# The gate stage of a product-key expert layer: one of its two one-hot products made by ScalarE instead of VectorE

## The chip, the cores and the metric

The kernel runs on one core of a Trainium2 chip. The metric is the device time of one execution in microseconds. Three runs of the kernel before took 2521.78, 2525.56 and 2527.47 us; their median is 2525.56 us.

## The reference

The program runs two blocks of two layers each on 256 tokens of width 1024. The first block (gated delta rule, retention, SwiGLU) is not touched. Each layer of the second block mixes the tokens (a linear recurrence beside sparse attention) and then applies a layer of experts. Only the experts matter here:

```python
q = (xf @ wq).reshape(T, 8, 2, 128)
s = jnp.einsum('thcd,ckd->thck', q, subkeys)
sv, si = lax.top_k(s, 16)                      # 16 best of 128 keys, twice
cand = (sv[:, :, 0, :, None] + sv[:, :, 1, None, :]).reshape(T, 8, 256)
cv, ci = lax.top_k(cand, 16)
experts = ea * 128 + eb                        # 8 heads x 16 experts a token, of 16384
gate = softmax(cv)
act = gelu(einsum('cd,ced->ce', xc, u_tab[experts]))
y = einsum('ce,ced->cd', act * gate, v_tab[experts])
```

Every token picks 128 of 16384 experts. Its output is the sum over these experts of gelu(x . u) times the gate times v.

## The kernel before

160 of the 256 tokens (`DENSE`) are computed densely. All 16384 products x . u are made in 128 units of 128 experts each (`u_unit`), multiplied by a gate table that is zero where an expert was not picked, and multiplied by v in 128 further steps (`v_part`). One unit and one `v_part` step are eight fp32 products of 128x128 by 128x160 each (16 matmul records in the profile). Each reads 128x1024 fp32 weights, half of a 1 MB load by the SP queue into the tiles `raw` (3 buffers) or `ru` (2).

The other 96 tokens (`FEW`) are computed by gathering the rows of u and v that they picked: `few_tokens` issues indirect DMAs from GpSimd, 128 rows of 1024 fp32 at a time (called a row batch below), into a ring of five tiles `frow`. VectorE reduces each u batch against x (line 1589) and adds each v batch to a sum (line 1595), and the tile is then free for the next gather. A layer has 192 such batches: 96 of u, then 96 of v.

The layer goes through these stages:

- Scores and first units: ten units are made ahead (`FIRST`).
- Ranks and top k: VectorE finds the experts; `pace` weaves units between.
- Gate stage (`gbuild`, line 1830): 40 steps of four tokens ("quads"). In a step VectorE writes two one-hot tables (`gAB`, line 1838: 128 picks in partitions, 128 first keys and 128 second keys in columns, four tokens innermost), and then the second one-hot times the gate (`gB2`, line 1840). The gate is held as two fp16 numbers, a high half and the remainder, so `gB2` has two halves. TensorE multiplies the first one-hot by both halves (line 1850: eight matmuls a quad), which sums the gates into a 128x128 table a token in PSUM. This is done one step late (`late`). VectorE (line 1857) multiplies the units that are already made by that table, and ScalarE (line 1859) copies the rest of the table out, to be multiplied when the unit comes.
- In each step `pace(self.QUAD)` runs `both`: one row batch, and then as many units as fit. A counter `spare` grows by `QUAD` and falls by `UNIT` = 2.2 with each unit; units are made while it is above zero. A unit in this stage is finished by a gelu on ScalarE (lines 1564 and 1567, split where the table already stands) and a product on VectorE (line 1565).
- V stage (in `peer_units`): 128 `v_part` steps (line 1666). The units that are still missing are spread over the first 96 steps, and the row batches over all steps, except the last eight (`HELD`). Then `peer_end` transposes the dense result, adds the sums of the gathered tokens (line 1712) and normalizes.

The order of instructions on each engine is fixed when the program is built. It follows the program's order, but a planner with its own costs lets an instruction go ahead where an earlier one is not ready by its reckoning. `tc.issue_after(self.mark)` keeps a row batch's VectorE instruction behind the quad's `gB2`.

Of the kernel before, what the change touches and what calls it, by code (L numbers as in the profile page):

```python
# [221 lines left out]
F32 = mybir.dt.float32  # L222
# [4 lines left out]
AF = mybir.ActivationFunctionType  # L227
ALU = mybir.AluOpType
# [25 lines left out]
class Body:  # L254
# [1220 lines left out]
    RANK = 1.0  # L1475
    TOP = 1.3
    DEC = 5.0
    QUAD = 2.2

    def peer(self, l):  # L1480

        nc, tc, I = self.nc, self.tc, self.I
        N, FEW = self.DENSE, self.FEW
        with tc.tile_pool(name="pz", bufs=1) as Z:
            self.few_pool = Z
            hk = Z.tile([128, 4, N], F16, name="hk")
            hf = Z.tile([128, 8, 256], F32, name="hf")
            groups = []  # L1490
            for g, (n, first) in enumerate(FEW):
                few = Z.tile([128, n], U32, name=f"fidx{g}")
                fg = Z.tile([128, n], F32, name=f"fgate{g}")
                fs = Z.tile([128, n], F32, name=f"fs{g}")
                fx = Z.tile([128, 1024], F32, name=f"fx{g}", tag=f"fx{g}")
                pair = Z.tile([128, n], F32, name=f"fpair{g}")
                if n == 64:
                    nc.vector.tensor_add(pair, self.ident[:, 0:64], self.ident[:, 64:128])
                else:
                    nc.vector.tensor_reduce(pair, self.ident.rearrange("p (r n) -> p n r", n=n), axis=mybir.AxisListType.X,  # L1500
                                            op=ALU.add)
                groups.append((n, first, few, fg, fs, fx, pair))
            sums = {}
            self.x_to_h(hf)
            with tc.tile_pool(name="pt", bufs=1) as P, tc.tile_pool(name="pm0", bufs=1) as M:
                prod = [M.tile([128, self.SPLIT, N], F32, name="prod0")]

                def u_products(w):
                    p = self.ps([128, N])
                    for k in range(8):  # L1510
                        nc.tensor.matmul(p, w[:, k * 128:(k + 1) * 128], hf[:, k, 0:N], start=(k == 0), stop=(k == 7))  # L1511
                    return p

                with tc.tile_pool(name="uf", bufs=self.FIRST // 2) as UF:
                    early = []

                    def ahead(i):
                        if i % 2 == 0 and 4 <= i < 4 + self.FIRST:
                            early.append(self.load_pair(I["pu"][l, (i - 4) // 2], UF))

                    with tc.tile_pool(name="hlw", bufs=2) as self.HL, tc.tile_pool(name="psw", bufs=2) as W:
                        best, rest = self.scores(l, P, W, ahead, prod[0].rearrange("p b t -> p (b t)")[:, -2048:])
                        self.settle()
                        for n, first, few, fg, fs, fx, pair in groups:
                            for s in range(0, 128, n):
                                nc.scalar.activation(fx[s:s + n, :], self.X[first:first + n, 1, :], AF.Copy)
                        for b in range(self.FIRST):
                            nc.scalar.activation(prod[0][:, b, :], u_products(early[b // 2][:, b % 2, :]), AF.Gelu_apprx_tanh)
                with tc.tile_pool(name="pm", bufs=1) as M:
                    prod.append(M.tile([128, 128 - self.SPLIT, N], F32, name="prod1"))  # L1530
                    self.peer_units(l, P, M, groups, sums, hk, u_products, best, rest, prod)
            with tc.tile_pool(name="pe", bufs=1) as W:
                self.peer_end(l, W, groups, sums)
# [284 lines left out]
    def turn(self, W, out, hk, ti, n):  # L1818


        nc = self.nc
        p = self.ps([128, 3, 128], "a")
        for z in range(3):
            nc.tensor.transpose(p[:, z, :], out[:, z, :], self.ident)
        t = slice(ti * 128, ti * 128 + n)
        nc.scalar.activation(hk[:, 0:2, t], p[:, 0:2, 0:n], AF.Copy)
        nc.scalar.activation(hk[:, 2, t], p[:, 2, 0:n], AF.Copy, scale=GATE_UNIT)
        nc.vector.scalar_tensor_tensor(hk[:, 3, t], p[:, 2, 0:n], GATE_UNIT, hk[:, 2, t], op0=ALU.mult, op1=ALU.subtract)

    def gbuild(self, W, iota4, hk, prod, state, pace):  # L1830

        nc, SPLIT = self.nc, self.SPLIT
        late = None
        for quad in range(self.DENSE // 4):
            t = slice(quad * 4, quad * 4 + 4)
            AB = W.tile([128, 2, 128, 4], F16, name="gAB")
            B2 = W.tile([128, 2, 128, 4], F16, name="gB2")
            nc.vector.tensor_tensor(AB, iota4[:, None].to_broadcast([128, 2, 128, 4]),
                                    hk[:, 0:2, None, t].to_broadcast([128, 2, 128, 4]), op=ALU.is_equal)
            self.mark = nc.vector.tensor_tensor(B2, AB[:, 1, None].to_broadcast([128, 2, 128, 4]),  # L1840
                                                hk[:, 2:4, None, t].to_broadcast([128, 2, 128, 4]), op=ALU.mult).ins
            if late is not None:
                late()
            pace(self.QUAD)

            def late(AB=AB, B2=B2, t=t):
                p = self.ps([128, 4, 128], "a")
                for j in range(4):
                    for i in range(2):
                        nc.tensor.matmul(p[:, j, :], AB[:, 0, :, j], B2[:, i, :, j], start=(i == 0), stop=(i == 1))  # L1850
                pv = p.rearrange("p t b -> p b t")
                made = state["made"]
                for i, (lo, hi) in enumerate(((0, SPLIT), (SPLIT, 128))):
                    m = min(max(made, lo), hi)
                    if m > lo:
                        d = prod[i][:, 0:m - lo, t]
                        nc.vector.scalar_tensor_tensor(d, pv[:, lo:m, :], 1.0 / GATE_UNIT, d, op0=ALU.mult, op1=ALU.mult)
                    if m < hi:
                        nc.scalar.activation(prod[i][:, m - lo:hi - lo, t], pv[:, m:hi, :], AF.Copy, scale=1.0 / GATE_UNIT)
                state["built"] = t.stop  # L1860
        late()
# [99 lines left out]
```

## Time and profile before

| | us |
|---|---|
| median of three runs | 2525.56 |
| profiled execution | 2522.34 |
| its span, first to last instruction | 2520.5 |
| TensorE busy | 2395.2 |
| VectorE busy | 1634.2 |
| ScalarE busy | 794.1 |
| GpSimd busy | 443.6 |

The span leaves out 1.84 us of the execution's own time. Matmuls are pipelined and their ends are modelled, so that the starts of TensorE's instructions tell its pace better than their lengths do. The two expert layers' gate stages lie at about 1129 to 1257 us and 1967 to 2090 us of the span, their V stages at 1257 to 1658 us and 2090 to 2497 us.

### The profile page before, as it was taken

The page shows a single profiled execution, that of the slowest core. Times are in us where ns is not written, and L with a number is a line of the kernel's source. Part 1 is how long each engine was busy: PE and PEld are TensorE (multiplying, and loading weights), DVE is VectorE, ACT ScalarE, POOL GpSimd, SP SyncE. Part 2 cuts the span into 40 slices and gives each one's busy share as a digit, 9 for nine tenths or more (in the row PEclk, how much of TensorE's full clock was granted, in tenths as well). Part 3 has the DMA queues.
Part 4 walks back from the last instruction along what each step waited for, and adds up shares of the span by engine and source line. Part 5 has one row for each costly group of instructions (what it writes and reads, how often), then busy time and mean ns, then how long its engine had stood idle before and what let it go on. Part 6 is the DMA issues. An engine that isn't in the chain of part 4 may idle for free. (4 is left out here: it accounts for less than half of the span.)

```text
span 2520.5 us, 42374 instructions
## 1 busy us (share of the span) xinstructions
PE 2395.2 (95%) x16994; PEld 2254.1 (89%) x16994; DVE 1634.2 (65%) x3427; ACT 794.1 (32%) x1653; POOL 443.6 (18%) x425
## 2 busy tenths in 40 slices
PE   5998999999999999999999999979999999999996
PEld 4887998977899887999999999958799999999995
DVE  6877886745555566989944444466589795444445
ACT  5464444344444456522200000034753220000000
POOL 0000000000000000033333233420002333333343
PEclk8999999999999999999999999989999999999998
DMA  7735996444455623579999999983265999999997
GB/s 289 254 132 198 328 333 240 152 163 163 144 198 184 198 89 132 200 298 333 330 397 415 412 415 406 407 294 114 86 236 216 349 336 375 415 415 416 413 406 296
DMA packets 153781, 704.38 MB, mean 279 GB/s; under 512 B 14704, under 2 KB 15600, under 8 KB 120176
## 3 DMA queue, kind: packets, MB, share of 16 engines
q1 hardware_dynamic: 97712, 498.43, 52.8%
q0 software_dynamic: 55296, 201.35, 20.7%
q8 instruction: 134, 2.20, 0.3%
q10 hardware_dynamic: 576, 1.89, 0.2%
q14 instruction: 63, 0.52, 0.1%
HBM read 700.57 MB, written 1.05 MB: 278 GB/s over the span
## 5 line engine op out<-in xcount | busy, mean ns | idle before, releaser
L1666 PE MATMUL ps_a<-prod,raw 128*128 128x160 f32 x4096 | 576.8, 299 | 7.4 <-DMA raw<-in_pv_dram 6.1
L1666 PEld LDWEIGHTS ps_a<-prod,raw 128*128 128x128 f32 x4096 | 562.7, 190 | 9.3 <-issue 6.8
L308 DVE TENSOR_TENSOR wlo<-raw,whi 128x1024 fp32r<-128x1024 f32 x316 | 385.5, 1223 | 249.2 <-ACT whi L306 245.1
L306 ACT ACTIVATE whi<-raw 128x1024 fp32r<-128x1024 f32 x316 | 333.2, 1058 | 389.1 <-PE ps_r L331 162.8
L1595 DVE SCALAR_TENSOR_TENSOR fa<-frow,fs,fa 128x1024 f32<-128x1024 f32 x188 | 241.5, 1284 | 277.9 <-DMA frow<-in_pv_dram,fidx 269.2
L330 PE MATMUL ps_r<-hh,whi 128*128 128x256 f32 x1376 | 393.6, 287 | 6.2 <-ACT whi L306 2.4
L331 PE MATMUL ps_r<-hh,whi 128*128 128x256 f32 x1376 | 390.8, 284 | 3.1 <-DVE hh L437 2.5
L332 PE MATMUL ps_r<-hh,wlo 128*128 128x256 f32 x1376 | 390.0, 284 | 2.6 <-DVE wlo L308 2.6
L1511 PE MATMUL ps_r<-hf,ru 128*128 128x160 f32 x2560 | 373.2, 299 | 0.0
L1511 PEld LDWEIGHTS ps_r<-hf,ru 128*128 128x128 f32 x2560 | 356.0, 190 | 0.1
L1589 DVE SCALAR_TENSOR_TENSOR frow<-frow,fx 128x1024 f32<-128x1024 f32 x192 | 233.7, 1220 | 126.4 <-DMA frow<-in_pur_dram,fidx 126.1
L1577 POOL DMA_INDIRECT frow<-in_pur_dram,fidx x192 | 208.2, 1084 | 571.0 <-DVE frow L1589 268.3
L1564 ACT ACTIVATE gelu<-ps_r 128x160 f32<-128x160 f32 (+10 forms) x192 | 53.0, 277 | 700.8 <-PE ps_r L1511 661.3
L330 PEld LDWEIGHTS ps_r<-hh,whi 128*128 128x128 f32 x1376 | 263.3, 192 | 10.2 <-ACT whi L306 2.9
L331 PEld LDWEIGHTS ps_r<-hh,whi 128*128 128x128 f32 x1376 | 263.5, 191 | 8.1 <-DVE hh L437 6.0
L332 PEld LDWEIGHTS ps_r<-hh,wlo 128*128 128x128 f32 x1376 | 263.1, 191 | 3.9 <-DVE wlo L308 3.8
L1577 POOL DMA_INDIRECT frow<-in_pv_dram,fidx x192 | 195.0, 1016 | 360.8 <-DVE fa L1595 186.0
L1511 PE MATMUL ps_r<-hf,raw 128*128 128x160 f32 x1536 | 225.2, 304 | 7.8 <-ACT prod L1567 6.1
L1511 PEld LDWEIGHTS ps_r<-hf,raw 128*128 128x128 f32 x1536 | 216.4, 194 | 8.9 <-ACT prod L1567 6.6
L1850 PE MATMUL ps_a<-gB,gAB 128*128 128x128 f16 x640 | 88.3, 295 | 0.0
L1565 DVE TENSOR_TENSOR prod<-prod,gelu 128x160 f32<-128x160 f32 (+10 forms) x192 | 55.4, 288 | 40.7 <-ACT gelu L1564 37.3
L1850 PEld LDWEIGHTS <-gAB 128*128 128x128 f16 x640 | 72.9, 116 | 2.6
(490 smaller groups left out, 3080.5 us busy)
## 6 DMA issues: line engine op xcount, KB each, us to landing
raw<-in_pv_dram SPq DMA_DIRECT2D x128, 1024.0 KB
ru<-in_pu_dram SPq DMA_DIRECT2D x80, 1024.0 KB
raw<-in_pu_dram SPq DMA_DIRECT2D x48, 1024.0 KB
raw<-in_ffn_in_dram SPq DMA_DIRECT2D x44, 1024.0 KB
adr<-in_ada_dram SPq DMA_DIRECT2D x56, 512.0 KB
raw<-in_ffn_out_dram SPq DMA_DIRECT2D x22, 1024.0 KB
raw<-in_ada_dram SPq DMA_DIRECT2D x20, 1024.0 KB
raw<-in_ret_tm_dram SPq DMA_DIRECT2D x16, 1024.0 KB
```

The costliest lines, as they stand in the source:

```text
L306: self.last_hi = self.nc.scalar.activation(hi[:, :n], src, AF.Copy)
L308: self.last_split = self.nc.vector.tensor_sub(lo[:, :n], src, hi[:, :n].bitcast(F32))
L330: nc.tensor.matmul(out, a, self.hhi[:, k, :], start=(k == 0), stop=False)
L331: nc.tensor.matmul(out, a, self.hlo[:, k, :], start=False, stop=False)
L332: nc.tensor.matmul(out, b, self.hhi[:, k, :], start=False, stop=(k == 7))
L1511: nc.tensor.matmul(p, w[:, k * 128:(k + 1) * 128], hf[:, k, 0:N], start=(k == 0), stop=(k == 7))
L1565: self.gated = nc.vector.tensor_mul(at(b)[:, 0:t], at(b)[:, 0:t], g[:, 0:t])
L1577: nc.gpsimd.indirect_dma_start(out=r, out_offset=None, in_=I["pv" if z else "pur"], in_offset=bass.IndirectOffsetOnAxis(groups[g][2][:, j: ...
L1589: nc.vector.scalar_tensor_tensor(r, r, 1.0, fx, op0=ALU.mult, op1=ALU.mult, accum_out=fs[:, j:j + 1])
L1595: nc.vector.scalar_tensor_tensor(fa, r, fs[:, j:j + 1], fa, op0=ALU.mult, op1=ALU.add)
L1666: nc.tensor.matmul(acc[c // 2][:, c % 2, :], v[:, c * 128:(c + 1) * 128], at(b), start=(b == 0 and c % 2 == 0), stop=(b == 127), skip_grou ...
L1850: nc.tensor.matmul(p[:, j, :], AB[:, 0, :, j], B2[:, i, :, j], start=(i == 0), stop=(i == 1))
```

## The change

`turn` also keeps the high half of the gate as fp32 (`hk2`, one more ScalarE copy in each of its two calls a layer). In `gbuild` VectorE makes only the low half of `gB2`. ScalarE makes the high half with four instructions a quad, one for each token: a copy of the second one-hot (128x128, every fourth element) with `hk2`'s column as the scale of each partition. `QUAD`, the pace of units, goes from 2.2 to 1.9.

```diff
-    QUAD = 2.2
+    QUAD = 1.9
...
             hk = Z.tile([128, 4, N], F16, name="hk")
+            self.hk2 = Z.tile([128, N], F32, name="hk2")
...
         nc.scalar.activation(hk[:, 2, t], p[:, 2, 0:n], AF.Copy, scale=GATE_UNIT)
+        nc.scalar.activation(self.hk2[:, t], hk[:, 2, t], AF.Copy)
...
-            self.mark = nc.vector.tensor_tensor(B2, AB[:, 1, None].to_broadcast([128, 2, 128, 4]),
-                                                hk[:, 2:4, None, t].to_broadcast([128, 2, 128, 4]), op=ALU.mult).ins
+            self.mark = nc.vector.tensor_tensor(B2[:, 1], AB[:, 1], hk[:, 3, None, t].to_broadcast([128, 128, 4]),
+                                                op=ALU.mult).ins
+            for j in range(4):
+                nc.scalar.activation(B2[:, 0, :, j], AB[:, 1, :, j], AF.Copy, scale=self.hk2[:, quad * 4 + j:quad * 4 + j + 1])
```

## Rows read from the trace of the kernel before

**Rows 1.** Page: busy time by engine, and what the DMA moved in 40 equal slices.
```profile
PE 2395.2 (95%) x16994; PEld 2254.1 (89%) x16994; DVE 1634.2 (65%) x3427; ACT 794.1 (32%) x1653; POOL 443.6 (18%) x425
...
GB/s 289 254 132 198 328 333 240 152 163 163 144 198 184 198 89 132 200 298 333 330 397 415 412 415 406 407 294 114 86 236 216 349 336 375 415 415 416 413 406 296
```

**Rows 2.** Windows: gate stage, two V stages. Columns: PE, PEld, DVE, ACT, POOL, PEclk, DMA, GB/s.
```profile
1129.30:1256.70 127.40, 127.40 (x982) 126.03 (x981) 115.20 (x263) 32.09 (x140) 44.25 (x40) 1.00 0.92 332
1256.70:1655.00 398.30, 394.67 (x2899) 393.61 (x2898) 182.98 (x243) 17.95 (x61) 133.01 (x134) 1.00 1.01 408
...
2090.00:2488.00 398.00, 394.24 (x2899) 393.36 (x2898) 184.84 (x251) 18.75 (x63) 137.24 (x135) 1.00 1.01 410
```

**Rows 3.** Chain of waits in time order: start, length, what held the chain.
```profile
1995.17 2.18 PE ps_r L1511 x16
1997.35 0.94 PE ps_a L1850 x8
...
2090.52 1.14 DVE frow L1589 x2
...
2252.97 13.09 DMA frow<-in_pv_dram,fidx
2266.16 1.28 DVE fa L1595
...
2503.00 4.93 PE ps_r L1712 x6
```

**Rows 4.** Timeline, first half of a gate stage: start, length, engine, instruction.
```profile
1175.24 0.69 DVE L1838 TENSOR_TENSOR gAB<-iota,hk 128x1024 f16<-128x1024 f16 x1
...
1176.37 0.68 DVE L1840 TENSOR_TENSOR gB<-gAB,hk 128x1024 f16<-128x1024 f16 x1
...
1178.37 0.69 DVE L1838 TENSOR_TENSOR gAB<-iota,hk 128x1024 f16<-128x1024 f16 x1
...
1178.83 1.11 PE L1850 MATMUL ps_a<-gB,gAB 128*128 128x128 f16 x8
```

**Rows 5.** Timeline, last third of the same gate stage, VectorE.
```profile
1241.10 0.30 DVE L1565 TENSOR_TENSOR prod<-prod,gelu 128x140 f32<-128x140 f32 x1
...
1244.21 0.31 DVE L1565 TENSOR_TENSOR prod<-prod,gelu 128x144 f32<-128x144 f32 x1
```

**Rows 6.** Groups by shape, VectorE: changed instruction, and 16-bit ones of other lengths.
```profile
L1840 DVE TENSOR_TENSOR gB<-gAB,hk 128x1024 f16<-128x1024 f16 x80 | 54.6, 682 | 0.0
...
L1807 DVE TENSOR_TENSOR teq<-teq 128x512 bf16<-128x512 bf16 x8 | 3.3, 417 | 0.0
...
L1807 DVE TENSOR_TENSOR teq<-teq 128x256 bf16<-128x256 bf16 x8 | 2.2, 280 | 0.0
```

**Rows 7.** Groups by shape, ScalarE: 128x128 without and with a per-partition operand.
```profile
L434 ACT ACTIVATE fmf<-ps_r,par 128x256 f32<-128x256 f32 x8 | 3.9, 575 | 1.4 <-PE ps_r L424 1.4
L830 ACT ACTIVATE vb<-ps_a,gbv 128x128 f32<-128x128 f32 x8 | 2.3, 367 | 0.0
L799 ACT ACTIVATE ktok<-ps_a,gbg 128x128 f32<-128x128 f32 x4 | 1.2, 408 | 0.0
L1827 ACT ACTIVATE hk<-ps_a 128x128 f16<-128x128 f32 x2 | 0.5, 271 | 0.0
```

**Rows 8.** Timeline: four ScalarE instructions with per-partition operands back to back.
```profile
1685.31 1.93 ACT L434 ACTIVATE fmf<-ps_r,par 128x256 f32<-128x256 f32 x4 [1.36 <-PE ps_r L424]
```

**Rows 9.** TensorE's waits in the two V stages and their ends.
```profile
PE ps_a L1666 <- DMA raw<-in_pv_dram: 3.0, 3, 1.9
...
PE ps_r L1712 <- DVE fa L1595: 4.7, 1, 4.7
PE ps_a L1666 <- DMA raw<-in_pv_dram: 3.1, 3, 2.1
```

**Rows 10.** Timeline, end of layer 0's V stage.
```profile
1650.67 7.84 PE L1666 MATMUL ps_a<-prod,raw 128*128 128x160 f32 x56 [1.91 <-DMA raw<-in_pv_dram]
...
1669.57 3.95 DVE L1595 SCALAR_TENSOR_TENSOR fa<-frow,fs,fa 128x1024 f32<-128x1024 f32 x3 [1.04 <-DMA frow<-in_pv_dram,fidx]
```

## The prediction

> **What bounds the kernel now.** I read the page first. TensorE is busy for 95% of the span, so whatever the change does elsewhere counts only through TensorE or through the ends of the two expert layers. The GB/s row shows the second thing to see: 333, 330 and 336 in the slices of the gate stages (19, 20 and 33), about 415 for the rest of both layers [rows 1]. Then I cut both layers into stages by windows. In layer 0's gate stage TensorE shows no idle time at all in 127.4 us, VectorE is busy for 115.2, ScalarE for 32.1, and DMA moves 332 GB/s. In the V stages TensorE is busy 394.7 of 398.3 and 394.2 of 398.0 us, DMA moves 408 to 410 GB/s, and its busy share is 1.01: both are full at once [rows 2].
>
> The chain of waits says which of the two ends last. Through the gate stage it runs on TensorE alone: 2.18 us for one unit of u, 0.94 us for a quad's eight gate matmuls. From 2090 us on it leaves TensorE for good and runs through the gathers: a gather takes 13.09 us to land, VectorE adds it in 1.28 us, that frees a ring tile, and so on to the last sum, which the pair product at 2503.00 waits for [rows 3]. Five tiles at 13.09 + 1.28 us give 2.87 us a row batch; the 144 batches that are left after the gate stage (192 less 40 in it and 8 before it) would take 414 us at that pace, and 2090 to 2503 is 413. So the end of a layer is the end of the gathers, and these are slow because the weights share a full DMA with them. The waits agree: TensorE waits 4.7 us for the last sum in layer 1, and 3.0 and 3.1 us for v weights [rows 9]. In layer 0 the last v product ends at 1658.5 and the last sum at 1673.5 [rows 10].
>
> **The change, part by part.**
>
> *Units.* From the code: 40 quads by 2.2 / 2.2 give 40 units in the gate stage; 40 by 1.9 / 2.2 = 34.5 give 35. Five units a layer move to the V stage, which then has 62 + 128 products instead of 57 + 128. At 2.18 us [rows 3] that takes 5 x 2.18 = 10.9 us of TensorE out of the gate stage and puts 10.9 us into the V stage: nothing for TensorE as a whole. Each unit brings its 0.524 MB weights along (128 x 1024 x 4 bytes), 2.62 MB a layer.
>
> *VectorE.* A quad's step was 3.13 us in the first half (start to start of line 1838 [rows 4]) and 3.11 us in the last third, where VectorE is packed [rows 5]. The halved product was not seen at its new size: it is 128x512 of fp16 instead of 128x1024 at 0.682 us. Bounds are 0.280 (128x256 bf16) and 0.682; the nearest is the 128x512 bf16 product, 0.417 [rows 6]. It saves 0.265 us a quad: 3.11 becomes 2.85 where VectorE is packed.
>
> *ScalarE.* Four instructions a quad of 128x128 with a scale per partition, SBUF to SBUF in fp16 with a stride, a form that no row shows. Without such an operand 128x128 takes 0.271 us, with one 0.367 to 0.408, so four cost 1.08 to 1.63 us [rows 7]. Back to back they overlap: four of 0.575 took 1.93 rather than 2.30 [rows 7, 8], so I take 4 x 0.367 less 3 x 0.12 = 1.1 us. ScalarE goes from 32.1 / 40 = 0.80 [rows 2] to about 1.9 us a quad, 2.4 at the upper bound, of a step of 2.85. It is not the bound, but 67 to 85% full and in order.
>
> Does the longer way to `gB2` delay the gate matmuls? They run one step late. The product of 1176.37 ends at 1177.05, its one-hot at 1175.93 [rows 4]; the matmuls that use it start at 1178.83 [rows 4]. ScalarE may begin at 1175.93 and needs 1.1 to 1.6 us, so it is done by 1177.6 with over a microsecond in hand. That hides it. Queued behind the four are the copy of the last table (line 1859) and the gelu of the unit, on which line 1565 on VectorE waits in order: where the four get in ahead of a gelu, VectorE stands still for up to 1.1 us. I count that at nothing on the mean, and it is the main risk. The extra copy in `turn`, some 0.3 us, twice a layer, is not in front of the one-hot, and units cover it.
>
> The Trainium skill speaks against the move: "ScalarE: Activation LUTs", section Rules for kernel authors, gives multiplications to VectorE rather than ScalarE. The rows agree as far as work goes (1.1 us added for 0.265 taken off); by that rule the step would lengthen wherever ScalarE is waited for, which is the slower rival below.
>
> *The gate stage.* TensorE needs 0.94 + 35/40 x 2.18 = 2.85 us a quad, VectorE 2.85 at its fullest. 40 quads took 127.4 us [rows 2]; less 10.9 it is 116.5 (2.91 a quad).
>
> *The V stage and the sum.* The gathers start their 144 batches 10.9 us earlier. Against that, DMA has 2.62 MB more to move while it is full: 2.62 MB / 415 GB/s [rows 1] = 6.3 us. Net -4.6 us a layer: the gain is DMA time that the gate stage left unused. If the planner lets units run ahead (of 982 matmuls in the gate stage [rows 2] 320 are the quads', and 662 make 41.4 units, not 40), and twice as many do so after, 3.6 units instead of 5 leave: 7.8 - 4.5 = -3.3 us a layer. Two layers give -9.2 to -6.6; I take the middle, -7.9. The profiled execution (span 2520.5, with 1.84 us around it 2522.34) would go to about 2514.4. It lay 3.2 us under the median, so against the median I say 2525.56 - 7.9 = 2517.7.
>
> **The rivals.**
>
> *Nothing moves (2525.6, 2522 to 2529).* TensorE is 99% busy or more in each window [rows 2], and the change takes no matmul away. The planner places row batches by the count of products made, so gathers may be held to TensorE's pace and start no batch earlier. Against it: VectorE waits for gathers, not the other way, and the chain from 2090 on does not touch TensorE [rows 3].
>
> *The gate stage does not get shorter (slower, 2538).* VectorE waits in order for a gelu behind the four, or the gate matmuls wait for the high half, and the step stays at 127.4 / 40 = 3.19 us with fewer units in it. Then 6.3 us of DMA a layer are added and nothing returned: +12.6, 2538. Were TensorE the bound in the V stage it would be +21.8, 2547. The point where it turns is a gate stage 6.3 us shorter, 121.1 us, 3.03 us a quad: a mean stall of 0.12 us over my 2.91 undoes the gain. For it: both engines are near 2.85 together, and ScalarE over two thirds full. Against it: matmuls of later units can fill TensorE, as they did before.
>
> *The gathers take it all (faster, 2507).* If weights go on at the old share of DMA, gathers end 10.9 us sooner in layer 0, where there is 15 us between last v product and last sum [rows 10], and up to 4.7 + 3.1 us sooner in layer 1 [rows 9]: -18.7, 2507.
>
> **How the numbers follow.** My forecast (-5 to -13) has 0.48, no change 0.22, the stage that does not shorten 0.22, the gathers that take all 0.08. About 0.2%, 5 us, is what a measurement of this kernel tells from no change. Faster is the first but 0.01 at its edge, with the last, 0.55; within 0.2% is the second and that edge, 0.23; slower is the third, 0.22. The likeliest case alone spans 2512 to 2521. The range for 8 in 10 goes from the last rival's 2507 to 2533, which takes in no change and the first part of the slower case and leaves the rest of it out.
>
> **What the profile after would show.** Right: line 1840 near 0.42 us, ScalarE's four near 0.37 each, matmuls of line 1850 about 2.9 us from quad to quad, the gate stages 8 to 11 us shorter with TensorE still without idle time, 62 gelus in each V stage, and v waits on weights no longer than before. Wrong: idle time before line 1850 released by ScalarE, VectorE waiting for gelu by tens of microseconds, quads at 3.03 us or more; or a shorter gate stage with the last sum where it was, which would say that the gathers do not set the end.

## The result and the profile after

The changed kernel takes 2499.29 us (median of five runs, 2494.03 to 2501.72), against 2525.56 us before (2521.78 to 2531.53 over five runs): a ratio of 0.9898, 95% interval 0.9884 to 0.9913. That is 26 us less, where 7.9 were forecast, and below the forecast's range of 2507 to 2533. The profiled execution took 2501.52 us, with a span of 2499.7.

The page of the changed kernel shows the trade that was meant, and one thing more: the chain that ended last has changed hands. The first line is busy time by engine, the second what DMA moved in 40 slices, the third the chain's share of the span by engine, and the last two are groups of instructions (count, busy time in us, mean of one in ns, then the engine's idle time before them).

```profile
PE 2387.4 (96%) x16994; PEld 2247.0 (90%) x16994; DVE 1609.7 (64%) x3421; ACT 897.7 (36%) x1971; POOL 491.9 (20%) x425
...
GB/s 290 253 135 194 328 319 254 154 160 162 161 183 175 216 87 100 254 251 354 342 410 416 414 415 415 390 303 128 89 242 215 371 338 399 415 414 415 414 390 306
...
PE 20%; DVE 3%; DMA 2%; issue 1%; ACT 0%; POOL 0%; POOLq 0%; DVEq 0%
...
L1566 DVE TENSOR_TENSOR prod<-prod,gelu 128x160 f32<-128x160 f32 (+9 forms) x192 | 56.8, 296 | 367.9 <-ACT gelu L1565 357.7
...
L1845 ACT ACTIVATE gB<-gAB,hk 128x128 f16<-128x128 f16 x320 | 121.0, 570 | 19.7 <-DVE gAB L1840 17.2
```

Before, the chain's shares were:

```profile
DMA 12%; PE 8%; DVE 4%; issue 2%; POOL 1%; ACT 0%; POOLq 0%; DVEq 0%; ACTq 0%
```

ScalarE gained 103.6 us of work and VectorE lost 24.5 [rows 1]. TensorE, which computes the same, was busy 7.8 us less: its matmuls themselves ran faster somewhere. DMA moves 354 and 342 GB/s in the slices of layer 0's gate stage (the second reaches 7 us into the V stage), where it moved 333 and 330 [rows 1].

The windows of the changed kernel, gate stage and V stage of each layer (columns as in [rows 2]):

```profile
1126.00:1242.90 116.90, 116.90 (x902) 114.44 (x902) 103.82 (x256) 81.14 (x291) 42.05 (x40) 1.00 0.94 348
1242.90:1656.40 413.50, 409.16 (x3008) 408.31 (x3007) 189.58 (x254) 20.43 (x67) 168.13 (x139) 1.00 1.01 408
1950.00:2066.90 116.90, 116.90 (x903) 114.44 (x902) 103.65 (x255) 81.12 (x291) 42.57 (x40) 1.00 0.93 348
2066.90:2479.30 412.40, 409.12 (x3006) 408.17 (x3006) 191.14 (x255) 20.25 (x67) 166.54 (x139) 1.00 1.01 406
```

The gate stage takes 116.9 us instead of 127.4 [rows 2], still without idle time on TensorE. Its matmuls are 902 less 320 of the quads: 582, or 36.4 units, five fewer than before.

One quad of it in the timeline (start, length, engine, instruction):

```profile
1174.18 0.69 DVE L1840 TENSOR_TENSOR gAB<-iota,hk 128x1024 f16<-128x1024 f16 x1
...
1175.19 1.50 ACT L1845 ACTIVATE gB<-gAB,hk 128x128 f16<-128x128 f16 x4
...
1175.34 0.42 DVE L1842 TENSOR_TENSOR gB<-gAB,hk 128x512 f16<-128x512 f16 x1
...
1177.79 1.10 PE L1854 MATMUL ps_a<-gB,gAB 128*128 128x128 f16 x8
```

ScalarE's four end at 1176.69, and the matmuls that use them start 1.1 us later, as in the working of the prediction. The step is mostly still 3.12 us where it holds a unit; steps without one are shorter, and there are more of them.

The end of layer 0's V stage, in the timeline of the changed kernel:

```profile
1648.56 7.84 PE L1667 MATMUL ps_a<-prod,raw 128*128 128x160 f32 x56 [2.57 <-DMA raw<-in_pv_dram]
...
1662.72 1.28 DVE L1596 SCALAR_TENSOR_TENSOR fa<-frow,fs,fa 128x1024 f32<-128x1024 f32 x1 [2.55 <-DMA frow<-in_pv_dram,fidx]
```

The last v product ends at 1656.4, the last sum at 1664.0: a tail of 7.6 us that was 15.0 [rows 10]. In layer 1 the chain of waits says the same. It stays on TensorE until the last unit, where before it had gone over to the gathers at 2090 [rows 3]:

```profile
2383.65 4.35 PE ps_a L1667 x32
2387.99 2.19 PE ps_r L1512 x16
...
2390.78 1.29 DVE fa L1596
...
2409.27 13.63 DMA frow<-in_pv_dram,fidx
2422.99 1.30 DVE fa L1596
...
2484.10 3.04 PE ps_r L1713 x6
```

And the waits of VectorE and ScalarE in layer 0's V stage, from 1242.9 to 1656.4 us (in total, times, longest): VectorE waits for the next unit's gelu, and the gelu for TensorE.

```profile
ACT gelu L1565 <- PE ps_r L1512: 309.8, 60, 8.1
DVE prod L1566 <- ACT gelu L1565: 176.5, 60, 3.9
...
DVE fa L1596 <- DMA frow<-in_pv_dram,fidx: 44.9, 26, 4.7
```

Before, it waited for gathers in that stage (here from 1250 to 1640 us) and hardly for a unit:

```profile
DVE fa L1595 <- DMA frow<-in_pv_dram,fidx: 119.6, 68, 3.7
...
DVE frow L1589 <- DMA frow<-in_pur_dram,fidx: 70.0, 39, 2.5
...
DVE prod L1565 <- ACT gelu L1564: 7.1, 2, 4.0
```

Read off the two profiled executions, the stages are (us; the gate stage is counted from its first matmul to the first v product, so that layer 1's ended at 2093.9 before; "tail" is from the end of the last v product to the end of the last sum):

| | before, layer 0 / 1 | after, layer 0 / 1 |
|---|---|---|
| first gate matmul at | 1129.5 / 1966.5 | 1126.1 / 1949.9 |
| gate stage | 127.4 / 127.4 | 116.8 / 116.8 |
| first gate matmul to last v product | 529.0 / 528.9 | 530.3 / 529.4 |
| tail | 15.0 / 7.5 | 7.6 / 4.8 |
| first gate matmul to last sum | 544.1 / 536.5 | 537.9 / 534.1 |

From the first gate matmul to the last sum the two layers lose 6.2 and 2.4 us, 8.6 together: the forecast's -9.2 to -6.6. But the first gate matmul itself comes 3.4 us earlier in layer 0, ahead of everything that the forecast counted. So two questions were open: what shortens the time before the gate stage, and whether the end of a layer is really set by gathers that want DMA time.

### The profile page after: what moved, and what is told of

It reads as the page before. It is cut to its first block, busy times and chain, and to the rows that moved or that the text cites. A ratio compares the mean times of both kernels' runs of the same rounds, so it can differ in the third digit from the quotient of the medians.

```text
span 2499.7 us, 42716 instructions
## 1 busy us (share of the span) xinstructions
PE 2387.4 (96%) x16994; PEld 2247.0 (90%) x16994; DVE 1609.7 (64%) x3421; ACT 897.7 (36%) x1971; POOL 491.9 (20%) x425
## 5 line engine op out<-in xcount | busy, mean ns | idle before, releaser
L1512 PE MATMUL ps_r<-hf,ru 128*128 128x160 f32 x2624 | 387.7, 299 | 0.0
L1512 PEld LDWEIGHTS ps_r<-hf,ru 128*128 128x128 f32 x2624 | 366.4, 190 | 0.2
L1578 POOL DMA_INDIRECT frow<-in_pur_dram,fidx x192 | 221.4, 1153 | 526.2 <-DVE frow L1590 292.0
L1578 POOL DMA_INDIRECT frow<-in_pv_dram,fidx x192 | 230.2, 1199 | 339.6 <-DVE fa L1596 289.0
L1565 ACT ACTIVATE gelu<-ps_r 128x160 f32<-128x160 f32 (+9 forms) x192 | 54.1, 282 | 671.2 <-PE ps_r L1512 663.1
L1566 DVE TENSOR_TENSOR prod<-prod,gelu 128x160 f32<-128x160 f32 (+9 forms) x192 | 56.8, 296 | 367.9 <-ACT gelu L1565 357.7
L1512 PE MATMUL ps_r<-hf,raw 128*128 128x160 f32 x1472 | 218.8, 300 | 4.7 <-ACT prod L1568 2.8
L1512 PEld LDWEIGHTS ps_r<-hf,raw 128*128 128x128 f32 x1472 | 205.0, 191 | 6.4 <-ACT prod L1568 3.3
L1845 ACT ACTIVATE gB<-gAB,hk 128x128 f16<-128x128 f16 x320 | 121.0, 570 | 19.7 <-DVE gAB L1840 17.2
L1854 PE MATMUL ps_a<-gB,gAB 128*128 128x128 f16 x640 | 99.3, 292 | 0.0
```

The costliest lines, as they stand in the source:

```text
L1578: nc.gpsimd.indirect_dma_start(out=r, out_offset=None, in_=I["pv" if z else "pur"], in_offset=bass.IndirectOffsetOnAxis(groups[g][2][:, j: ...
L1845: nc.scalar.activation(B2[:, 0, :, j], AB[:, 1, :, j], AF.Copy, scale=self.hk2[:, quad * 4 + j:quad * 4 + j + 1])
```

## The experiments

The expectations call the second point theory G: the gathers, sharing a full DMA with the weights, set the end of a layer, and a shorter gate stage gives them an earlier start. Against it stand that pace or split alone does it, and that the order in which batches are issued holds them back. For the first point the suspect was the copy in `turn` (theory T), against scatter between executions. All kernels were timed in five rounds, in three groups, each beside the kernel before (2525.73, 2526.22 and 2524.69 us there).

### The copy alone

```diff
+            self.hk2 = Z.tile([128, N], F32, name="hk2")
...
+        nc.scalar.activation(self.hk2[:, t], hk[:, 2, t], AF.Copy)
```

This is the kernel before with a tile that nobody reads.

> The kernel before with nothing but the extra ScalarE copy of the gate's high half in `turn`; the copy is read by nobody. Theory T (table load): the copy takes over the wait of the softmax's exp for ScalarE's own earlier work, so that the table load before exp no longer waits for VectorE and runs in ScalarE's idle time; TensorE's pause before the gate stage goes from 3.0 to 1.4 us in both layers, its clock does not fall behind it, and both gate stages start 2 to 4 us earlier: 6 to 9 us faster, about 2518. Rival D (VectorE's freed time does it all): the same time as before, 2525, within 3 us.

Measured: 2516.85 us, 0.9968 (0.9957 to 0.998). An added instruction, read by nobody, makes the kernel 8.9 us faster. Its traces show how. In `topk` ScalarE loads a table before the softmax's exp, and another before the next gelu. ScalarE in the kernel before, layer 0:

```profile
1090.02 0.30 ACT L1567 ACTIVATE prod<-ps_r 128x160 f32<-128x160 f32 x1 [1.87 <-PE ps_r L1511]
1098.42 1.28 ACT L1811 ACT_TABLE_LOAD   x1 [8.10 <-DVE tout L1788]
1099.71 0.31 ACT L1811 ACTIVATE tout<-tout 128x128 f32<-128x128 f32 x1
1100.04 1.28 ACT L1567 ACT_TABLE_LOAD   x1
1101.34 0.89 ACT L1567 ACTIVATE prod<-ps_r 128x160 f32<-128x160 f32 x4
```

ScalarE in the kernel with the copy alone:

```profile
1089.68 0.30 ACT L1568 ACTIVATE prod<-ps_r 128x160 f32<-128x160 f32 x1 [1.87 <-PE ps_r L1512]
1090.00 1.28 ACT L1812 ACT_TABLE_LOAD   x1
1097.78 0.31 ACT L1812 ACTIVATE tout<-tout 128x128 f32<-128x128 f32 x1 [6.49 <-DVE tout L1789]
1098.10 1.28 ACT L1568 ACT_TABLE_LOAD   x1
1099.40 0.89 ACT L1568 ACTIVATE prod<-ps_r 128x160 f32<-128x160 f32 x4
```

Without the copy the table load waits 8.10 us for VectorE, together with the exp behind it; with it the load runs at the start of that wait. The semaphores say why. A trace keeps which one each instruction waits for; for a table load it keeps none, so that its wait is read from the rows above. By the engine that raises the semaphore, the same in both layers:

```
before   ACT_TABLE_LOAD                       VectorE (read from the rows)
         ACTIVATE tout<-tout (exp)            ScalarE
copy     ACTIVATE hk2<-hk                     ScalarE
         ...
         ACT_TABLE_LOAD                       none (read from the rows)
         ACTIVATE tout<-tout (exp)            VectorE
```

So the exp of the kernel before depended on two engines, VectorE and ScalarE itself for its earlier work, and the wait for VectorE stood at the table load. The copy reads `hk`, which ScalarE has just written, and waits for ScalarE's own work; afterwards the exp waits only for VectorE, and the load no longer waits. All gelus queue behind the exp and the second load, so 1.28 us there is 1.28 us more in which no PSUM tile comes free. TensorE in the kernel before, layer 0 and layer 1:

```profile
1101.69 14.00 PE L1511 MATMUL ps_r<-hf,raw 128*128 128x160 f32 x80 [3.02 <-ACT prod L1567]
...
1939.94 12.81 PE L1511 MATMUL ps_r<-hf,raw 128*128 128x160 f32 x80 [3.09 <-ACT prod L1567]
```

TensorE in the kernel with the copy alone:

```profile
1099.75 11.13 PE L1512 MATMUL ps_r<-hf,raw 128*128 128x160 f32 x80 [1.42 <-ACT prod L1568]
...
1931.48 11.13 PE L1512 MATMUL ps_r<-hf,raw 128*128 128x160 f32 x80 [1.40 <-ACT prod L1568]
```

The pause is 1.6 and 1.7 us shorter, and the 80 matmuls behind it are 2.87 and 1.68 us shorter. The second part is the clock. In the 15 us after the pause, the granted clock (third column from the end) of the kernel before is a mix of its two levels, 1.2 and 2.4 GHz:

```profile
1101.60:1116.60 15.00, 14.91 (x88) 14.91 (x89) 13.68 (x23) 2.15 (x9) 9.24 (x7) 0.80 0.83 270
1939.90:1954.90 15.00, 14.96 (x98) 14.96 (x99) 14.53 (x27) 2.10 (x8) 9.60 (x8) 0.89 0.84 285
```

In the changed kernel it is 1.00, with 110 matmuls in the same time rather than 88:

```profile
1101.70:1116.70 15.00, 14.95 (x110) 14.95 (x111) 13.89 (x26) 2.41 (x9) 10.19 (x7) 1.00 0.85 311
```

Together 4.5 us in layer 0 and 3.4 in layer 1, 7.9 of the 8.9 measured (5.1 to 10.9 by the interval).

### The change with the copy taken from PSUM

```diff
-        nc.scalar.activation(self.hk2[:, t], hk[:, 2, t], AF.Copy)
+        nc.scalar.activation(self.hk2[:, t], p[:, 2, 0:n], AF.Copy, scale=GATE_UNIT)
```

The copy now reads what TensorE wrote, so it carries no wait for ScalarE; its trace shows no wait on it at all.

> The changed kernel, but the fp32 copy is made from PSUM instead of from the fp16 high half, so that it waits for TensorE and not for ScalarE. Theory T: the table load before exp waits for VectorE again, the pause of 3.0 us and the lower clock behind it come back: 6 to 9 us slower than the changed kernel, about 2506, 18 to 20 us faster than before. Rival D: as the changed kernel, 2499.

Measured: 2502.66 us, 0.9905 (0.9891 to 0.992), 3.4 us above the changed kernel, with intervals that overlap, where 6 to 9 were expected. The order came back as it was before, and the exp waits for ScalarE's semaphore again:

```profile
1092.71 0.30 ACT L1568 ACTIVATE prod<-ps_r 128x160 f32<-128x160 f32 x1 [1.87 <-PE ps_r L1512]
1100.84 1.28 ACT L1812 ACT_TABLE_LOAD   x1 [7.83 <-DVE tout L1789]
1102.14 0.31 ACT L1812 ACTIVATE tout<-tout 128x128 f32<-128x128 f32 x1
```

So did the pause, 2.75 us in both layers; the clock fell behind it in layer 1 only:

```profile
1104.12 11.13 PE L1512 MATMUL ps_r<-hf,raw 128*128 128x160 f32 x80 [2.75 <-ACT prod L1568]
...
1924.74 12.81 PE L1512 MATMUL ps_r<-hf,raw 128*128 128x160 f32 x80 [2.75 <-ACT prod L1568]
```

The wait is what the copy changes: with another wait on the same copy, the table load, the pause and in one layer the clock go back. What that costs here is not clear of the scatter; the price of 8.9 us is that of the copy alone. The pause is shorter than in the kernel before, and the clock did not always fall. Over the thirteen profiled kernels, eight pauses at this place took 2.75 to 3.13 us, and seven of them were followed by a lower clock (80 matmuls in 12.73 to 14.08 us); eighteen took 1.40 to 1.84 us, and none was (11.13 us each).

### Pace alone, and split alone

```diff
-    QUAD = 2.2
+    QUAD = 1.9
```

> The kernel before with QUAD 1.9 and VectorE's product left whole. Theory G (the gathers share a full DMA set and end last, so a shorter gate stage lets them start sooner): VectorE's 3.1 us a quad keep the gate stage near 120 to 125 us, five units more go to the V stage: between 4 us faster and 10 us slower, about 2528. Rival R (only the number of units in the stage matters, TensorE being packed in it): gate stage 10 us shorter, 2513.

The second kernel is the changed one with `QUAD` put back to 2.2.

> The changed kernel with QUAD 2.2: the product is split, the pace is as before. Theory G with T: TensorE's 3.12 us a quad keep the gate stage at 125 us, so only the table load's 6 to 9 us are gained: 2518. Rival D (the freed VectorE time is what pays): 2500 to 2506.

Measured: pace alone 2521.61 us (0.9978, 0.9964 to 0.9993), with runs from 2509 to 2530 and the profiled one, 2527.14, near their upper end; split alone 2510.97 (0.9936, 0.9923 to 0.9949), 14.8 us faster, of which the copy makes 8.9 if it is worth there what it is alone (the pauses are 1.40 and 1.41 us there too). That lies between the two expectations for it, 2518 and 2500 to 2506. Neither part does all of it. With pace alone VectorE's quads stay as long as they were. The two windows are the gate stages of that kernel:

```profile
1132.20:1259.90 127.70, 124.15 (x943) 122.04 (x942) 113.00 (x256) 30.57 (x131) 50.04 (x40) 0.99 0.91 331
1970.60:2096.80 126.20, 122.96 (x944) 120.85 (x943) 113.00 (x255) 30.43 (x131) 49.80 (x40) 1.00 0.91 332
```

They take about as long as before, now with 3.6 and 3.2 us in which TensorE is idle (2.6 of the 3.6 in one wait for u weights); it makes 943 less 320 matmuls, 38.9 units, in them, only 2.5 fewer than before. Where the 4 us of this kernel's median come from, its trace does not show. With split alone VectorE is quick enough, but all 40 units are still made there, though no longer 41.4: 124.6 us, and no idle time. The 2.8 us less in each layer come near what split alone gains beyond the copy. Together the stage is 116.8 us, and the kernel gains 26, more than the 4 and 15 of its parts.

### Gathers thinned out, before and after

```diff
-            order = [(z, g, j) for z in range(2) for g in range(len(groups)) for j in range(groups[g][0])]
+            order = [(z, g, j) for z in range(2) for g in range(len(groups)) for j in range(groups[g][0]) if not (z and j % 2)]
...
-        rows, asked, last = 2 * sum(n for n, *_ in groups) - taken[0], 0, []
+        rows, asked, last = 3 * sum(n for n, *_ in groups) // 2 - taken[0], 0, []
```

Both kernels without every second batch of gathered v rows: 48 of a layer's 192 batches are left out.

> The kernel before, leaving out every second batch of gathered v rows (48 of a layer's 192 batches; the output of 96 tokens lacks those experts). Theory G (the end of a layer is the last gathered sum, late because gathers and weights share a full DMA set): without them the last sum comes at most 5 us after the last v product instead of 15.0 and 7.5, and TensorE no longer waits for v weights (3.5 us a layer): 15 to 22 us faster than before, about 2506. Rival O (the last batches are late because of their place in VectorE's order): the two gaps stay at 10 us or more, within 8 us of before.

> The changed kernel, leaving out the same batches. Theory G: it gains only what is left of its own gaps (7.6 and 4.8 us) and of its waits for weights: 8 to 13 us faster than the changed kernel, about 2489, and its lead over the thinned kernel before is only the table load's and what lies between the layers, 8 to 14 us instead of 26. Rival O: the lead stays above 20 us.

Measured: 2495.84 us (0.9879, 0.9864 to 0.9895) and 2489.57 (0.9854, 0.9839 to 0.9869). The kernel before gains 30 us by it, more than the 15 to 22 that I expected, the changed one 10. In both the last sum now comes 11 to 14 us ahead of the last v product, and the chain is on TensorE nearly throughout; the thinned kernel before:

```profile
PE 23%; DVE 2%; DMA 1%; ACT 0%; issue 0%; DVEq 0%; ACTq 0%
```

With the gathers out of the way the change is worth 6.3 us, somewhat less than the 8 to 14 expected and about what the copy alone gave. So most of the rest of its 26 us goes through the gathers, as theory G has it.

Thinning takes VectorE's sums away too, so by itself it does not say what makes the gathers late. The traces do. In the kernel with the copy alone a gather lands in a median of 7.4 us in layer 0's gate stage (1125 to 1250 us), where DMA moves 336 GB/s, and in 13.1 us (rows of v) or 13.9 (rows of u) in its V stage (1260 to 1640), through the same ring of five tiles, where DMA moves 412. In the thinned kernel before it moves 361 in that stretch. VectorE, busy for 183 of 398 us in the V stage [rows 2], waits 120 us in total for gathers that have not landed.

### A still lower pace

```diff
-    QUAD = 1.9
+    QUAD = 1.6
```

> The changed kernel with QUAD 1.6: 29 or 30 units in the gate stage instead of 35. Theory G: the gathers start up to 8 us earlier still, and the gaps after the last v product shrink by a few us, while VectorE (about 2.65 us a quad) now bounds the stage: 2494 to 2500. Rival S (ScalarE, at 81 of 117 us, delays the gate matmuls as soon as fewer units cover them): TensorE idle in the gate stage by 5 us or more, 2503 to 2510.

Measured: 2505.01 us (0.9914, 0.9897 to 0.9932), with runs from 2499 to 2512. That is no gain over 1.9, and by the medians a loss of 6 us, though the intervals overlap; it lies in the range of rival S (2503 to 2510), not in that of theory G (2494 to 2500). The profiled execution was the slowest. The gate stages shrink by little more and TensorE begins to idle in them:

```profile
1124.70:1239.20 114.50, 112.65 (x867) 108.84 (x865) 101.37 (x246) 79.91 (x282) 48.30 (x40) 1.00 0.94 344
1956.00:2071.50 115.50, 112.64 (x866) 108.83 (x865) 101.44 (x247) 79.98 (x282) 48.86 (x40) 1.00 0.92 342
```

They hold 34.1 units and come to 2.86 and 2.89 us a quad, near the 2.85 that the prediction gave VectorE at its fullest. TensorE idles for 1.9 and 2.9 us in them, most of it until ScalarE is done and 1.1 us for u weights, less than the 5 us in a stage that rival S names. What TensorE idles here it has to make up behind: the way from the first gate matmul to the last v product is 531.6 and 533.6 us instead of 530.3 and 529.4.

### The last batches issued earlier in the order, and the repeat

```diff
-    HELD = 8
+    HELD = 0
```

`HELD` is the number of a layer's last row batches that are not spread over the V stage but stand behind it. The changed kernel with 0:

> The changed kernel with HELD 0: the last eight row batches of a layer are spread over the V stage instead of standing behind it. Theory G with a V stage that now has DMA time to spare: the gaps of 7.6 and 4.8 us go to 2 to 4 us, 4 to 8 us faster than the changed kernel, about 2493. Rival F (DMA is as full as before): TensorE waits for v weights by as much more, 2499.

The changed kernel again, unaltered:

> The changed kernel once more, beside the two that follow, to see how much of its lead is scatter from run to run. Theory G with T: 2499 within 3 us, 0.989 to 0.991 of before; the gap after the last v product 8 and 5 us; the stage between the layers (attention) is not touched by the change and takes 205 to 208 us.

With `HELD = 4`:

> The changed kernel with HELD 4. Theory G with DMA time to spare in the V stage: gaps of 3 to 5 us instead of 7.6 and 4.8, 2 to 5 us faster than the changed kernel, 2495 to 2497, the fastest of all. Rival F (DMA still full, what the gathers win the v weights lose): the same as the changed kernel within 2 us.

And the copy alone with `HELD = 0`:

> The kernel before with the extra copy alone (2517 earlier) and HELD 0. Theory G (gathers late for want of DMA time, not by their place in the order): moving eight batches forward on paper does not make them land sooner, so that TensorE or the end waits as long: 2513 to 2519. Rival O (the place in the order is what makes them late): the gaps of 14.5 and 9.5 us go to 3 us as in the changed kernel with HELD 0, 2500.

Measured: 2497.95 (0.9892, 0.9877 to 0.9907), 2496.48 (0.9897, 0.9882 to 0.9912), 2496.61 (0.9891, 0.9876 to 0.9906) and 2515.11 us (0.9965, 0.9953 to 0.9977). The repeat gives the changed kernel's ratio again. On the changed kernel 0 and 4 bring the tails to 2 us and below, yet the time is the same within the intervals: the 4 to 8 and 2 to 5 us that theory G expected did not come, and the time fits rival F, by which it stays the same, though TensorE's waits for v weights did not grow as F has it (7.6 us in the two layers after and in the repeat, 8.5 with 0, 7.1 with 4). On the copy alone `HELD = 0` brings the tails from 14.5 and 9.5 us to no less than 10.2 and 9.7, and no gain clear of scatter (2515.11 against 2516.85): its gathers are late for want of DMA time, not by their place in the order. No version that gathers all rows is shown to beat the changed kernel.

## Why the prediction was wrong

**The bound (right).** Gathers that share a full DMA set the end of a layer before; thinning them takes 30 us off. The forecast missed the other side of it: once they have caught up, TensorE sets the end, and in the changed kernel the chain is back on it for most of the V stage.

**Units, VectorE, ScalarE, the gate stage (right).** Five units moved, at almost no cost to TensorE: 529.0 and 528.9 us before, 530.3 and 529.4 after, from the first gate matmul to the last v product. The low half's product took 418 ns, 417 were taken. ScalarE's four took 1.5 us, 1.1 were taken and 1.63 was the upper bound; a single one took 570 ns, outside its own bounds, and the overlap made up for most of it. The gate stage went to 116.8 us, forecast 116.5.

**The V stage and the sum (near it in the traces, low by the medians).** Working from the end of the gate stage to the last sum, before took 416.7 and 409.1 us, after 421.1 and 417.3: 12.6 us more in two layers, where the added weights were priced at 6.3 a layer; the repeat's trace gives 9.4. The agreement is in part luck: it was 4.4 us in layer 0 and 8.2 in layer 1 (repeat 0.5 and 8.9), not 6.3 in each. In layer 1 the tail was only 7.5 us before, and TensorE, with its work unchanged, left no more than that to gain. The sum leaves -8.6 us (repeat -11.8) where -7.9 was forecast.

**The copy in `turn` (the step that failed).** The prediction put it at "some 0.3 us", "not in front of the one-hot", covered by units, and so at nothing. It looked at what the instruction occupies, not at what it waits for. By taking over a wait it freed a table load of 1.28 us to run while ScalarE idled, shortened a pause of TensorE and with that kept its clock: 8.9 us by itself. The row that could have warned was in the trace of before: a table load with 8.10 us of idle time ended by VectorE, in front of an exp with none. With the copy alone the same load ran 7.8 us ahead of its exp, so what it had waited for was the exp's business, not its own. With these 8.9 us the forecast would have been 2508.8, and the measured time still 9.5 below it.

**The rest.** With the copy set apart (2516.85), the change takes 17.6 us more off the medians. From the trace of the copy alone to that of the changed kernel (repeat in brackets), the two layers from the first gate matmul to the last sum lose 9.7 us (13.0), the way between them 2.6 (3.3) and the end of the program behind the last sum 2.7 (2.6). The last two are terms that the prediction did not have.

They go with the length of the tail, in which TensorE idles. In the six profiled kernels with a tail of 9.9 to 15.0 us in layer 0, the granted clock fell from 2.4 to 1.2 GHz in the tail, and twice more some 60 and 110 us into the next layer's attention stage; that stage took 206.9 to 208.0 us. In the seven with a tail of 7.6 us or less, or none, it fell there once or not at all, and the stage took 203.5 to 206.5 us: 207.8 before, 206.9 with the copy alone, 204.7 after, 203.7 with `HELD = 0` and 203.5 with `HELD = 4`. These are single executions, and no run changes the clock by itself, so the link is seen but not shown to be the cause.

The profiled pair differs by 20.8 us where the medians differ by 26.3, since single executions scatter by 8 to 10 us. By the medians the third rival, gathers that take it all (2507), plus the copy would come to 2498, close to the 2499 measured; by the traces of the layers the forecast's own price for DMA comes nearer. Which of these a typical execution follows was not settled.

**The rivals.** Nothing moves: refuted by the ratio. The stage that does not shorten: refuted, though pace alone shows such a stage (126 to 128 us with fewer units), without the loss of 12.6 us that was priced, by the median. The stall that it named stayed small. VectorE's waits for ScalarE in the gate stage of the changed kernel's layer 0:

```profile
DVE prod L1566 <- ACT prod L1863: 4.6, 12, 0.7
...
DVE prod L1566 <- ACT gelu L1565: 3.5, 9, 0.6
```

That is 8.1 us over 40 quads, 0.2 us each, in a stage in which TensorE never idled. The 357.7 us in the page's line for line 1566 lie in the V stages, where the wait is for the next unit.

## What to carry to other kernels

Price an added instruction by its waits too: one that makes an engine wait for its own earlier work, or for a neighbour, takes that wait off whatever comes later, and a table load may then slip into idle time. Work taken off a stage with free DMA into one without it costs the bytes that it brings along; it pays only if the stage really shortens, so the pace and the load on its fullest engine have to be changed together. When two limits end nearly at once, removing the later one is worth only the distance to the other.

## What the runs showed of the hardware

- A ScalarE copy of 128x128 fp16 from SBUF to SBUF, every fourth element, with a scale per partition, takes 549 to 596 ns, and four back to back take 1.49 to 1.50 us, some 0.31 each beyond the first. The Trainium skill, "ScalarE: Activation LUTs", section What ACT_TABLE_LOAD costs, gives 186 ns and 0.833 ns an element, with some 93 ns more for a pointer operand: 386 ns, as an estimate by it. The trace doesn't agree for this form.
- A table load took 1.28 us, and the next instruction started right behind it, at 1099.71 after one at 1098.42. The same section of the Trainium skill's "ScalarE: Activation LUTs" counts a drain of about 1.38 us on top for each switch; the rows of ScalarE shown here have no room for it.
- A pause of TensorE of 3.0 to 3.1 us in the kernel before cost another 2.87 and 1.68 us by the clock: 80 matmuls took 14.00 and 12.81 us behind it, and 11.13 behind a pause of 1.4.
- A gather of 128 rows of 4 KB landed in a median of 7.4 us while DMA moved 336 GB/s in all, and in 13.1 to 13.9 us while it moved 412 (copy alone, layer 0).
